# Full-width operands, ScalarE copies and closed chain visits in the RWKV stage of a decoder layer

## The chip, the cores and the metric

The kernel runs on one core of one Trainium2 chip. The metric is the device time of one execution in microseconds (us). The time before is 2257.15 us, the median of 3 runs (2256.23 to 2258.58).

## What is computed

One decoder layer on 1024 tokens of 1024 channels, in float32. One wide input projection of the normalised input feeds three branches and three gates per channel; the branches are merged, projected, and followed by a gated feed-forward network with a short convolution.

```python
h = rms_norm(x, norm_mix_pre)
z_pool, z_q, z_rwkv, z_gate = split(h @ w_in)        # 512, 512, 3328, 3072 columns
y_pool = pool_branch(z_pool) @ w_proj_pool           # causal means over 2, 4, 8, 16 tokens
y_mem  = mem_attention(z_q, mem, w_mem_kv) @ w_proj_mem   # 4 heads, 256 memory tokens
y_rwkv = rwkv_branch(token_shifted(z_rwkv)) @ w_proj_rwkv # 16 heads of 64 channels
merged = g0 * y_pool + g1 * y_rwkv + g2 * y_mem      # g = sigmoid(z_gate + gate_b)
x = x + rms_norm(merged @ w_o)
x = x + rms_norm(conv_ffn(rms_norm(x)))              # 1024 -> 2 x 2816 -> 1024

# rwkv_branch, for each head and token:
sa    = state @ an
state = state * w + outer(sa, bn) + outer(v, k)      # an = -kk, bn = kk * a
y     = state @ r
```

The RWKV recurrence over 1024 tokens is computed in 16 chunks of 64 tokens. Inside a chunk the recurrence becomes matrix products and the inverse of a triangular 64x64 matrix; between chunks the state is handed on.

## The kernel before

**Dense products.** Every float32 product is made of three fp32r matmuls (`mm3`, L158 to L163): operands are split into a high and a low part, and hi·hi, hi·lo and lo·hi are added in one accumulator. A block of the input projection (`in_block`, L249) is 128 output channels for all tokens: two halves of 512 tokens, eight input slices of 128, three matmuls each, so 48 matmuls of 128x512. Its weights come by DMA (`load_w`, L139), 128x256 at a time; `split_w` (L122) writes the high part, either on ScalarE (L124) where `hi_on_act` is set or on GpSimd (L126), and GpSimd subtracts for the low part (L127). Three raw and four split tiles of each class are kept in turn.

**Stages.** `start` (L316) makes the first blocks and the output gate of the RWKV branch. Then come four calls of `rwkv_group` (L376), one for each group of two pairs of heads (i = 0, 1; a pair fills 128 channels). After the groups: the keys and values of the memory, the attention (L643 to L714), the pool branch (L718 to L751), the projections of the three branches with the merge, the output projection, and the feed-forward network.

**A group.** Its parts, in the order of the program:
- preparation (L390 to L446): sigmoids of two low-rank products (psu, L398), the squared norm of the keys by a product with a matrix of ones for each head (`head_sums` L363, phd), a scan on VectorE, two exponentials, the block of r, then the operands AR (three planes: -kk decayed, r decayed, and a plane used by halves) and BK (L425 to L436, each by halves of 64 partitions), and the bonus r·k times v (pbo, L442), which goes to memory at L445;
- centred values (pv, L453 to L461);
- chunk products ps1 and ps2 (L469 to L489): 4 chunks a bank, two banks in turn, each read by three VectorE operations with a mask (L480 to L482, L487 to L489) into RB, NT and AR;
- BK times the chunk's decay Dc, one VectorE operation of 128x2048 for each pair (L491), transposes of it (pt) into BKN (L493 to L497);
- a recursion of 31 steps on VectorE that inverts 32x32 triangles (L513 to L518), between transposes (L510, L519, L520), then copies of the result into NT (L521 to L526), and the products pz and pw (L529 to L543) that join the halves of each 64x64 inverse;
- the chain of 16 chunks (L549 to L590). For each chunk: pr from the state (L554, L555), copied to Rs by VectorE (L557); pu = NT times Rs (L560, L561), copied to HV by VectorE and ScalarE (L566, L567); ph, the next state (L571, L572), added to the decayed one by VectorE (L577) for the next chunk; the output py in two parts, one that needs only the state (L564, L565) and one that needs pu (L586, L588), copied by ScalarE (L590). Each of these sets is eight small matmuls, 64 wide;
- the blocks of k and v of the next group (`group_kv`, L354), and the head norm of the outputs (pvar, L595 to L613).

**Order of the work.** Each engine runs a queue of its own. A scheduler orders the instructions of every engine by data, by free buffers and by their place in the program; `later` (L199) adds an order between two instructions without a wait of its own. The blocks that nobody in the groups needs (4 of the pool, 4 of the queries, 24 of the gates) stand in a list `fill`; the first 24 are written in the program behind the four groups, the last 8 in the pool stage (L739 to L741, two for each of the four pool groups gi). The scheduler takes their matmuls forward as filling wherever TensorE would have nothing to do.

**Pool stage.** For each gi: load z (tz, one buffer, so one gi after the other), window sums on VectorE over 128x1024 (L729 to L738), split into zh and zl for each half, three matmuls with the split pool weights (psg from zh, uhi), bias and scale, split again into ph_ and pl_, which the projection of the branch reads later.

## Time and profile before

| | us |
|---|---|
| median of 3 runs | 2257.15 |
| profiled execution: time | 2256.94 |
| profiled execution: span, first to last instruction | 2255.2 |
| TensorE busy | 2155.7 (96%) |
| VectorE busy | 1176.7 (52%) |
| ScalarE busy | 837.1 (37%) |
| GpSimd busy | 766.4 (34%) |
| mean granted clock of TensorE | 0.982 |

The profile is of one execution; its 2256.94 us lies 0.2 us below the median, and 1.7 us of it lie outside the span. A busy TensorE is not one at its peak: small matmuls, and matmuls at a lower clock, count as busy too. So the argument goes by three things: idle time of TensorE in front of a group of instructions and what released it, the distance from the start of one matmul to the start of the next, and the granted clock of a stretch.

### The profile page before, as it was taken

Reading aid. Unit: us, or ns where it says so; the run is one execution under the profiler, and the core shown is the slowest. Engines: PE = TensorE matmul, PEld = TensorE weight load, DVE = VectorE, ACT = ScalarE, POOL = GpSimd, SP = SyncE. Lnnn points to the kernel's source line nnn. Section 1 sums busy time; section 2 is a strip of 40 time slices with the busy share of each in tenths; the row PEclk is TensorE's granted clock in tenths of the full one; section 3 lists DMA queues with packets and bytes.
Section 4 is the critical chain, followed back from the end, with each engine's and each line's share of the span. In section 5 each row is a group of like instructions: output and inputs, shape, how many; then the busy total and the mean of one; then the engine's idle time right before and its main releaser. Section 6 shows DMA issues by size and latency. Waiting matters only on the chain.

```text
span 2255.2 us, 34230 instructions
## 1 busy us (share of the span) xinstructions
PE 2155.7 (96%) x12630; PEld 1649.1 (73%) x12630; DVE 1176.7 (52%) x2101; ACT 837.1 (37%) x1696; POOL 766.4 (34%) x1025
## 2 busy tenths in 40 slices
PE   7999899989998999899989999999999999999998
PEld 4767566766676667667877878777888888888887
DVE  6277539653965386634764442767403423334237
ACT  3342234223432252224634244545433413323143
POOL 6552116222521242212153355556422222323240
PEclk9999999999998999999999999999999999999999
DMA  4311112112111121114336343543211111111123
GB/s 138 126 54 50 38 60 68 57 39 67 66 55 41 54 92 44 57 56 142 98 117 201 130 145 100 163 153 94 76 50 45 50 50 42 54 40 57 38 75 136
DMA packets 147319, 181.46 MB, mean 80 GB/s; under 512 B 15824, under 2 KB 115792, under 8 KB 147152
## 3 DMA queue, kind: packets, MB, share of 16 engines
q1 hardware_dynamic: 147152, 179.28, 24.4%
q8 instruction: 100, 1.64, 0.3%
q14 instruction: 67, 0.55, 0.1%
HBM read 141.46 MB, written 37.75 MB: 79 GB/s over the span
## 4 chain that ended last, share of the span: by engine, by line
PE 73%; DVE 17%; DMA 3%; ACT 3%; issue 2%; POOL 2%; SPq 0%; POOLq 0%; ACTq 0%; DVEq 0%
PE psg L161 20%; PE psg L162 20%; PE psg L163 20%; DVE tb L518 2%; DVE tb L516 2%; PE ps L486 2%; PE ps L479 1%; POOL wlo L127 1%; PE pr L554 1%; PE pu L560 1%; ACT tHV L191 1%; DVE AR L425 1%; PE py L564 1%; PE py L586 1%; DMA wraw<-in_w_in 1%
## 5 line engine op out<-in xcount | busy, mean ns | idle before, releaser
L127 POOL TENSOR_TENSOR wlo<-wraw,whi 128x256 fp32r<-128x256 f32 (+1 forms) x696 | 578.3, 835 | 686.7 <-ACT whi L124 606.3
L161 PE MATMUL psg<-hh,whi 128*128 128x512 f32 x928 | 389.2, 420 | 0.9 <-ACT hh L117 0.7
L162 PE MATMUL psg<-hl,whi 128*128 128x512 f32 x928 | 386.6, 417 | 1.6 <-DVE hl L118 1.6
L126 POOL TENSOR_SCALAR whi<-wraw 128x256 fp32r<-128x256 f32 x240 | 151.3, 630 | 695.4 <-PE psg L162 671.9
L163 PE MATMUL psg<-hh,wlo 128*128 128x512 f32 x928 | 384.1, 414 | 0.2
L124 ACT CAST whi<-wraw 128x256 fp32r<-128x256 f32 (+1 forms) x488 | 191.8, 401 | 361.5 <-PE psg L162 274.2
L161 PE MATMUL psg<-h2h,whi 128*128 128x512 f32 x704 | 279.7, 397 | 4.4 <-DVE zc L826 4.4
L163 PE MATMUL psg<-h2h,wlo 128*128 128x512 f32 x704 | 278.7, 396 | 1.2 <-POOL wlo L127 1.2
L162 PE MATMUL psg<-h2l,whi 128*128 128x512 f32 x704 | 278.6, 396 | 0.0
L161 PEld LDWEIGHTS psg<-hh,whi 128*128 128x128 f32 x928 | 177.0, 191 | 47.0 <-issue 2.2
L163 PEld LDWEIGHTS psg<-hh,wlo 128*128 128x128 f32 x928 | 177.4, 191 | 43.2 <-issue 2.2
L162 PEld LDWEIGHTS psg<-hl,whi 128*128 128x128 f32 x928 | 177.0, 191 | 43.0 <-DVE hl L118 2.5
L161 PEld LDWEIGHTS psg<-h2h,whi 128*128 128x128 f32 x704 | 132.4, 188 | 37.3 <-ACT whi L124 5.0
L163 PEld LDWEIGHTS psg<-h2h,wlo 128*128 128x128 f32 x704 | 132.3, 188 | 34.2 <-POOL wlo L127 1.6
L162 PEld LDWEIGHTS psg<-h2l,whi 128*128 128x128 f32 x704 | 132.4, 188 | 32.7 <-issue 0.5
L823 DVE SCALAR_TENSOR_TENSOR uv<-psg,pv,uv 128x511 f32<-128x511 f32 x44 | 33.0, 749 | 156.7 <-ACT uv L822 156.7
L163 PE MATMUL psg<-fh,wlo 128*128 128x512 f32 x288 | 113.8, 395 | 0.0
L162 PE MATMUL psg<-fl,whi 128*128 128x512 f32 x288 | 113.8, 395 | 0.0
L161 PE MATMUL psg<-fh,whi 128*128 128x512 f32 x288 | 113.6, 395 | 0.0
L823 DVE SCALAR_TENSOR_TENSOR ug<-psg,pv,ug 128x511 f32<-128x511 f32 x44 | 32.9, 749 | 146.2 <-ACT ug L822 146.2
L989 DVE TENSOR_TENSOR acc<-acc,psg 128x512 f32<-128x512 f32 x48 | 33.0, 687 | 102.5 <-PE psg L163 102.5
L276 ACT ACTIVATE st<-psg,pv 128x512 f32<-128x512 f32 x48 | 33.1, 690 | 108.9 <-PE psg L163 99.1
(341 smaller groups left out, 3975.0 us busy)
## 6 DMA issues: line engine op xcount, KB each, us to landing
wraw<-in_w_in SPq DMA_DIRECT2D x240, 128.0 KB, 2.3
wraw<-in_w_fup SPq DMA_DIRECT2D x216, 128.0 KB, 2.3
d_zg<-st SPq DMA_DIRECT2D x48, 256.0 KB, 2.6
wraw<-in_w_fdn SPq DMA_DIRECT2D x80, 128.0 KB, 2.1
wraw<-in_w_prwkv SPq DMA_DIRECT2D x64, 128.0 KB, 2.3
wraw<-in_w_o SPq DMA_DIRECT2D x64, 128.0 KB, 2.3
xr<-in_xT SPq DMA_DIRECT2D x16, 256.0 KB, 5.4
d_g<-st SPq DMA_DIRECT2D x16, 256.0 KB, 2.0
```

What stands on the lines that cost most here:

```text
L124: A.copy(hi, src)
L126: G.tensor_scalar(hi, src, 1.0, 0.0, op0=ALU.mult, op1=ALU.add)
L127: (V if lo_on_dve[0] else G).tensor_tensor(lo, src, hi.bitcast(F32), op=ALU.subtract)
L161: first = PE.matmul(ps, wh, xh, start=start, stop=False)
L162: PE.matmul(ps, wh, xl, start=False, stop=False)
L163: last_mm[0] = PE.matmul(ps, wl, xh, start=False, stop=stop).ins
L276: A.activation(st, ps, AF.Identity, bias=bias)
L486: PE.matmul(ps[:, c], BK[i][up, c0 + c], AR[up, i, 1:3, t], start=True, stop=True)
L516: V.tensor_tensor(tm, X[:, s + 1:, s:s + 1].broadcast_to([P, n, m]), S[:, s:s + 1, 0:m].broadcast_to([P, n, m]), op=ALU.mult)
L518: V.tensor_tensor(S[:, s + 1:, 0:m], S[:, s + 1:, 0:m], tm, op=ALU.add)
L823: V.scalar_tensor_tensor(d[:, 1:], ps[:, :511], col("cw1", j), d[:, 1:], op0=ALU.mult, op1=ALU.add)
L989: V.tensor_tensor(accs[n][:, j], accs[n][:, j], ps, op=ALU.add)
```

## The change

Eight edits, all but two of them inside `rwkv_group`:

1. `square_sums` takes the place of `head_sums`: ScalarE writes the rounded square and the full square, two operations of 128x512 for each half, where it wrote one square of 128x1024 and VectorE rounded it.
2. The products for AR and BK are made for 128 rows in one operation (AR: 4 VectorE operations become 2; BK: 4 become 2, with one result first in t2), and ScalarE copies halves of 64 rows to where they are needed: one for AR and three for BK, for each pair.
3. `product_bank`: ps1 and ps2 take three banks in turn. RB is copied by ScalarE without the mask, and VectorE masks it later in four operations of 128x1024 in front of the chain. The bonus (pbo) moves behind the products of i = 0.
4. BK times Dc: 16 ScalarE operations of 128x128 for i = 0; 8 of them and a VectorE operation on the other half for i = 1.
5. `fill_to(95 * g + 95)`: six blocks of `fill` are written into each group in front of the NT copies. The order behind the recursion is moved: only the first pz matmul is ordered, behind the last NT copy of VectorE.
6. `visit`: the small matmuls of a chunk are tied together by `later`: pr with the first part of py, pu alone, ph with the second part of py. pr, pu and ph take two banks in turn.
7. `hi_on_act` is set after `start`, and stays: the high parts of nearly all weights are written by ScalarE (L124), where in the groups and in the pool stage GpSimd wrote them.
8. The 24 blocks behind the groups are gone (edit 5 has them), and the pool stage takes the 8 that are left, two for each gi as before.

The diff, cut to its core:

```diff
+    def square_sums(src, scale, sq):
...
-            V.tensor_copy(sp[:, n, 0], src[:, s])
-            V.tensor_tensor(sp[:, n, 1], src[:, s], sp[:, n, 0].bitcast(F32), op=ALU.subtract)
+            A.activation(sp[:, n, 0], src[:, s], AF.Square, scale=scale)
+            A.activation(sq[:, s], src[:, s], AF.Square, scale=scale)
+            V.tensor_tensor(sp[:, n, 1], sq[:, s], sp[:, n, 0].bitcast(F32), op=ALU.subtract)
...
+            A.copy(AR[64:128, i, 2], AR[64:128, i, 0])
             V.tensor_tensor(t5_, t5_, t4_, op=ALU.mult)
-            V.tensor_tensor(BK[0:64, :, 0:64], c3(t5_)[0:64], c3(t2_)[0:64], op=ALU.mult)
-            V.tensor_tensor(BK[64:128, :, 64:128], c3(t5_)[64:128], c3(t2_)[64:128], op=ALU.mult)
+            V.tensor_tensor(BK[:, :, 0:64], c3(t5_), c3(t2_), op=ALU.mult)
+            A.copy(BK[64:128, :, 64:128], BK[64:128, :, 0:64])
...
+            V.tensor_tensor(t2_, t4_, t2_, op=ALU.mult)
+            A.copy(BK[0:64, :, 64:128], c3(t2_)[0:64])
+            A.copy(BK[64:128, :, 0:64], c3(t2_)[64:128])
...
-                V.tensor_tensor(RB[i][:, 0, cs], ps[:, :, 1], bc(mincl, full), op=ALU.mult)
+                A.copy(RB[i][:, 0, cs], ps[:, :, 1])
...
-            V.tensor_tensor(BK[i], BK[i], Dc[:, i].unsqueeze(2).broadcast_to([P, NCH, P]),
-                            op=ALU.mult)
+            for b in range(2 if i == 0 else 0):
+                bonus(b)
+            n = NCH if i == 0 else 8
+            for c in range(n):
+                A.activation(BK[i][:, c], BK[i][:, c], AF.Identity, scale=Dc[:, i, c:c + 1])
...
-        behind = V.transpose(X.rearrange("p u t -> p t u"), S).ins
+        V.transpose(X.rearrange("p u t -> p t u"), S)
+        fill_to(95 * g + 95)
...
+        for i in range(2):
+            for e in range(2):
+                V.tensor_tensor(RB[i][:, e], RB[i][:, e], mincl.unsqueeze(1).broadcast_to([P, NCH, C]),
+                                op=ALU.mult)
...
+            visit(row, ready)
...
+    first_kv = start()
+    hi_on_act[0] = True
...
-    for j, ev in fill[:24]:
-        in_block(j, ev, 1)
...
-            n = 16 + 2 * gi
-            for j, ev in gates[n:n + 2]:
+            for j, ev in fill[2 * gi:2 * gi + 2]:
                 in_block(j, ev, 1)
```

How the orders of the engines move is shown at three places. **TensorE in the chain**, before: one chunk in the first group (hh, hl: the normalised input; psg: a dense block). The small sets stand in visits of their own between dense matmuls.

```order
L162 MATMUL psg<-hl,whi 128x512
L564 MATMUL py<-AR,HV 64x64
L565 MATMUL py<-AR,HV 64x64
L564 MATMUL py<-AR,HV 64x64
L565 MATMUL py<-AR,HV 64x64
L163 MATMUL psg<-hh,wlo 128x512
L554 MATMUL pr<-HV,AR 64x64
L555 MATMUL pr<-HV,AR 64x64
L554 MATMUL pr<-HV,AR 64x64
L555 MATMUL pr<-HV,AR 64x64
L161 MATMUL psg<-hh,whi 128x512
```

The same place of the change; here L589 is the line of `visit`, through which all the small matmuls go, and L161 to L163 are the dense ones as before:

```order
L162 MATMUL psg<-hl,whi 128x512
L589 MATMUL pr<-HV,AR 64x64 x4
L589 MATMUL py<-AR,HV 64x64 x4
L163 MATMUL psg<-hh,wlo 128x512
L589 MATMUL pu<-Rs,NT 64x64 x4
L161 MATMUL psg<-hh,whi 128x512
L162 MATMUL psg<-hl,whi 128x512
L163 MATMUL psg<-hh,wlo 128x512
L161 MATMUL psg<-hh,whi 128x512
L589 MATMUL ph<-HV,BKN_1303 64x64 x2
```

The first part of py now stands with pr in one visit; a chunk has three visits where it had four. The same table gives the number of dense matmuls between the last chunk product of a group and its first pz: 123 before, 226 in the first group and 211 to 213 in the others in the change.

**TensorE in the pool stage**, before, around the products of the third pool group (zh, zl): dense blocks of the input projection stand between them and after them.

```order
L161 MATMUL psg<-hh,whi 128x512
L161 MATMUL psg<-zh,uhi 128x512
L162 MATMUL psg<-hl,whi 128x512
L163 MATMUL psg<-hh,wlo 128x512
L162 MATMUL psg<-zl,uhi 128x512
L163 MATMUL psg<-zh,ulo 128x512
L161 MATMUL psg<-hh,whi 128x512
```

In the change, from the third pool group to the fourth (ph_, pl_: the finished pool outputs, read by the branch's projection; oh: the attention's output, read by its projection):

```order
L161 MATMUL psg<-zh,uhi 128x512
L162 MATMUL psg<-zl,uhi 128x512
L163 MATMUL psg<-zh,ulo 128x512
L161 MATMUL psg<-ph__9400,whi 128x512
L162 MATMUL psg<-pl__9401,whi 128x512
L163 MATMUL psg<-ph__9400,wlo 128x512
L161 MATMUL psg<-ph__9400,whi 128x512
L162 MATMUL psg<-pl__9401,whi 128x512
L163 MATMUL psg<-ph__9400,wlo 128x512
L161 MATMUL psg<-zh,uhi 128x512
```

From the first to the last of these pool products there were 192 matmuls of the input projection before and there is 1 in the change; 114 matmuls of the pool's projection are taken forward to there, and the last zh stands only six matmuls behind the third.

**ScalarE in the preparation of the second pair**, in the change, from the rounding of weights to the first chunk product's copy:

```order
L124 CAST whi<-wraw 128x256 x3
L438 COPY AR<-AR 64x1024
L444 ACTIVATE tHV<-tHV,oka,pv 128x1024
L442 COPY BK_5328<-BK_5328 64x16x64
L262 ACTIVATE AR<-psg,omu 128x512
L124 CAST whi<-wraw 128x256
L447 COPY BK_5328<-tBN_5325 64x16x64
L448 COPY BK_5328<-tBN_5325 64x16x64
L124 CAST whi<-wraw 128x256 x3
L262 ACTIVATE AR<-psg,omu 128x512
L497 COPY RB_5689<-ps_5709 128x256
```

Before, at the same place and up to the first copy of a centred value:

```order
L124 CAST whi<-wraw 128x256
L276 ACTIVATE st<-psg,pv 128x512
L433 ACTIVATE tHV<-tHV,oka,pv 128x1024
L276 ACTIVATE st<-psg,pv 128x512
L444 ACTIVATE kv_5784<-kv_5784,pv 128x1024
L460 COPY HV<-pv 64x8x64
```

Four copies of halves and the rounding of all weights have come into ScalarE's queue in front of the copies that free the product banks.

More of the change, by code (lines that the diff above doesn't have):

```diff
@@ L174, in gemm @@
                 later(m, behind)
+            if log is not None:
+                log.append(last_mm[0])
         return ps
@@ L401, in rwkv_group, with product_bank @@
         vs = []
+        turn = [0]
+        def product_bank(name):
+            turn[0] = (turn[0] + 1) % 3
+            shape = [P, 4, 2, C]
+            return pss.tile(shape, F32, name=name, tag="s") if turn[0] else \
+                psk.tile(shape, F32, name=name, tag="k")
         for i in range(2):
@@ L548, in rwkv_group, with bank, visit @@
         Hd = rw.tile([P, 2, C], F32, name="Hd", tag="Hd")
+        turn = [0]
+        def bank(name):
+            turn[0] ^= 1
+            return (psc if turn[0] else psk).tile([P, 2, C], F32, name=name, tag="c" if turn[0] else "k")
+        def visit(products, after):
+            for (out_, l, r), kw in products:
+                m = PE.matmul(out_, l, r, **kw)
+                if after is not None:
+                    later(m, after)
+                after = m.ins
+            return after
@@ L568, in rwkv_group @@
+            for i in range(2):
+                kw = dict(start=c == 0 and i == 0, stop=i == 1)
+                row.append(((py[lo, i], HV[:, i, c, 0], RB[i][:, 0, c]), kw))
+                row.append(((py[up, i], HV[:, i, c, 1], RB[i][:, 1, c]), kw))
+            visit(row, ready)
             if c + 1 < NCH:
-                ph = psc.tile([P, 2, C], F32, name="ph", tag="c")
-                for i in range(2):
-                    PE.matmul(ph[lo, i], BKN[i][:, c, 0:64], HV[:, i, c, 0], start=True, stop=True)
-                    PE.matmul(ph[up, i], BKN[i][:, c, 64:128], HV[:, i, c, 1], start=True, stop=True)
```

112 lines of the change are left out of this document (61 added, 51 removed).

## The prediction, on record before the run

> **What bounds the kernel now.** I read the page's busy shares first, then the busy time of each engine in the stretches of the groups, the groups of instructions with what ended the idle time before them, and TensorE's timeline at one place of each kind.
>
> ```profile
> PE 2155.7 (96%) x12630; PEld 1649.1 (73%) x12630; DVE 1176.7 (52%) x2101; ACT 837.1 (37%) x1696; POOL 766.4 (34%) x1025
> ```
>
> ```profile
> 113.00:339.00 226.00, 215.27 (x1728) 153.10 (x1728) 138.21 (x274) 75.44 (x152) 66.29 (x91) 0.98 0.15 50
> ...
> sum 902.00, PE 852.03 PEld 608.65 DVE 562.52 ACT 303.93 POOL 267.18; mean PE 213.01 PEld 152.16 DVE 140.63 ACT 75.98 POOL 66.79
> ```
>
> TensorE is busy for 96% of the span; no other engine passes 52%. The four stretches are one group's period each (chain to chain); in them TensorE idles 902.00 − 852.03 = 50 us. So a gain can come from idle TensorE time, from time that it is busy for badly, and from nothing else; a relieved VectorE is worth only what waits for it. The groups say what waits:
>
> ```profile
> L534 PE MATMUL pz<-tb,NT 32*32 32x32 f32 x512 | 12.5, 214 | 30.3 <-DVE tb L519 30.3
> L442 PE MATMUL pbo<-kv,bonesr 128*128 128x512 f32 x32 | 15.9, 618 | 12.6 <-DVE kv L438 12.6
> L398 PE MATMUL psu<-ld,ulo 128*128 128x512 f32 x16 | 6.9, 430 | 2.8 <-POOL ulo L313 2.8
> L161 PE MATMUL psg<-hh,whi 128*128 128x512 f32 x700 | 298.0, 426 | 0.1
> ```
>
> The end of VectorE's recursion (before pz) and the bonus's operand account for 42.9 of the 50 us; the dense matmuls wait for nothing. A gap also costs behind itself. This is TensorE behind the first recursion:
>
> ```profile
> 240.99 1.92 PE L534 MATMUL pz<-tb,NT 32*32 32x32 f32 x64 [7.46 <-DVE tb L519]
> ...
> 243.43 0.63 PE L162 MATMUL psg<-hl,whi 128*128 128x512 f32 x1
> 243.86 0.63 PE L163 MATMUL psg<-hh,wlo 128*128 128x512 f32 x1
> ```
>
> and the granted clock (the third number from the end) in the stretches there:
>
> ```profile
> 240.00:246.00 6.00, 5.01 (x72) 3.97 (x73) 5.00 (x7) 2.99 (x5) 1.23 (x2) 0.50 0.01 3
> 246.00:252.00 6.00, 6.00 (x138) 4.14 (x137) 2.27 (x5) 3.63 (x7) 1.14 (x2) 0.80 0.26 90
> ```
>
> Behind the 7.46 us gap the granted clock is 0.50, then 0.80 in the next 6 us, and dense matmuls start 0.43 us apart (243.43 to 243.86). Next, one chunk of the chain:
>
> ```profile
> 287.34 0.40 PE L162 MATMUL psg<-hl,whi 128*128 128x512 f32 x1
> 287.66 0.27 PE L564 MATMUL py<-AR,HV 64*64 64x64 f32 x1
> ...
> 288.06 0.50 PE L163 MATMUL psg<-hh,wlo 128*128 128x512 f32 x1
> 288.49 0.27 PE L554 MATMUL pr<-HV,AR 128*64 128x64 f32 x1
> ...
> 288.72 0.22 PE L555 MATMUL pr<-HV,AR 128*64 128x64 f32 x1
> 288.87 0.51 PE L161 MATMUL psg<-hh,whi 128*128 128x512 f32 x1
> 289.21 0.39 PE L162 MATMUL psg<-hl,whi 128*128 128x512 f32 x1
> 289.44 0.40 PE L163 MATMUL psg<-hh,wlo 128*128 128x512 f32 x1
> ```
>
> Dense matmuls in a run start 0.23 us apart (289.21 to 289.44). From 287.34 to 289.21 there are three dense steps, 0.70 us, and the visits of py and pr; so the two visits cost 1.87 − 0.70 = 1.17 us, though their 16 small matmuls start within 0.25 us of each other in each visit. The rest is the way in (0.09 more than a dense step), the way out (0.15, from 288.72 to 288.87) and a first dense step that is 0.11 too long (0.34).
>
> **The change part by part.** *Cover for the recursion (edit 5).* The last product eviction of the first group, and pz:
>
> ```profile
> 203.48 0.42 DVE L489 TENSOR_TENSOR AR<-ps,mstrict 64x256 f32<-64x256 f32 x1
> 203.82 2.27 DVE L491 TENSOR_TENSOR BK<-BK,Dc 128x2048 f32<-128x2048 f32 x1
> ```
>
> From 203.5 to 240.99 are 37.5 us, and TensorE had 123 dense matmuls for them by its order: 123 × 0.233 = 28.7 us and the transposes, 7.5 short, as the trace has it. The change puts 211 to 226 there, 49 to 53 us. The NT copies that now stand ahead of pz add some 3.5 us to the 37.5, so about 8 us remain to spare: the gap goes, −30.3 us. With it goes the slow clock: 5 us at 0.50 and 6 us at 0.80 lose 2.5 + 1.2 = 3.7 us at most; I take 3.0 a group, since the time to change modes may not scale with the clock: −12.
>
> *Bonus (edit 3).* pbo now stands behind the products of i = 0, long after its operand: −12.6 us. The short wait before psu goes with GpSimd's rounding of weights: −2.8, rounded to −3.
>
> *Visits (edit 6).* py's first part joins pr. What stays inside is a step from pr's matmuls (128x64) to py's (64x64). This trace shows that step where the two happened to meet:
>
> ```profile
> 328.12 0.22 PE L555 MATMUL pr<-HV,AR 128*64 128x64 f32 x1
> 328.27 0.27 PE L565 MATMUL py<-AR,HV 64*64 64x64 f32 x1
> ```
>
> 0.15 us, the same as the way out to a dense matmul. So a merged visit saves 0.09 + 0.15 + 0.11 of one visit and pays 0.15: 0.20 us, in 60 chunks (four groups, fifteen with a first py) −12 us. The Trainium skill, "TensorEngine Tiling (Array Packing)", Key Properties, says that a change of tiling mode drains the array while a change of tile does not. The row agrees that the switch inside the visit costs as much as one at its end; counted as if only visits cost, the saving would be 0.35 × 60 = 21 us. Elsewhere in the groups about 20 more switches go, at 0.15: −3.
>
> *What ScalarE takes over (edits 1 to 4, 7).* Its prices, and what VectorE and GpSimd give up:
>
> ```profile
> L126 POOL TENSOR_SCALAR whi<-wraw 128x256 fp32r<-128x256 f32 x171 | 106.7, 624 | 575.5 <-PE psg L162 558.7 <-issue 12.7 <-POOL ulo L313 1.9
> L124 ACT CAST whi<-wraw 128x256 fp32r<-128x256 f32 x4 | 1.6, 402 | 0.5 <-PE psg L162 0.5
> L480 DVE TENSOR_TENSOR RB<-ps,mincl 128x256 f32<-128x256 f32 x32 | 13.6, 425 | 54.2 <-PE ps L479 54.1
> L410 ACT ACTIVATE tHV<-kv,pv 128x1024 f32<-128x1024 f32 x6 | 6.9, 1152 | 0.0
> L584 ACT ACTIVATE Hd<-Hn,Dc 128x64 f32<-128x64 f32 x112 | 32.9, 340 | 34.8 <-DVE Hn L582 32.6 <-DVE Hn L580 2.2
> ```
>
> ```profile
> 330.00:397.00 67.00, 62.15 (x300) 44.97 (x299) 55.26 (x65) 34.23 (x49) 35.94 (x34) 0.97 0.22 78
> ```
>
> For each group: 43 roundings at 0.402 = 17 us; 16 copies of RB at 0.40 = 6.4; 8 copies of halves at 1.15 = 9.2; 24 scalings by Dc at about 0.34 = 8.2; squares +2.5. That is 43 us on top of 76 in a period of 225, so ScalarE is not full over a group. In the preparation it comes close: in the 67 us from 330 it had 34 and gets some 20 more, in a stretch that should itself shrink to about 60. VectorE is paid there: 16 evictions × 0.425 = 6.8 and the 2.27 us of L491 among others go, and four masks of 128x1024 come back.
>
> What this costs TensorE the trace of before doesn't show. From below it is nothing: TensorE's dense filling covers all of it. From above, every one of the 16 product banks of a group is freed late by two roundings that stand ahead of the copy, 16 × 0.8 = 13 us. I take half of the banks late by one rounding, 8 × 0.40 = 3.2, and two copies of halves (2 × 1.15 = 2.3) on the path from VectorE's operand to the first product: 5.5 us a group, +22. It lies nearer to nothing because three banks in turn give slack that two did not. The Trainium skill, "ScalarE: Activation LUTs", Rules for kernel authors, tells to keep plain multiplications on VectorE. By its about 0.3 us for each instruction and 0.83 ns for each element, my estimate for a 128x128 scaling is 0.41 us, 24 of them 9.8 us against the two VectorE operations that L491 measures at 2.27; no run here shows that shape, and the sum, by the row, has 8.2.
>
> *Pool stage (edits 5 and 8).* The filling is taken from here.
>
> ```profile
> 1141.00:1212.00 71.00, 65.42 (x262) 50.08 (x261) 41.50 (x55) 21.39 (x36) 40.71 (x45) 0.95 0.39 132
> ```
>
> ```profile
> 1141.98 0.69 DVE L118 TENSOR_TENSOR ol<-po,oh 128x512 fp32r<-128x512 f32 x1 [1.57 <-ACT oh L117]
> 1165.63 0.50 PE L161 MATMUL psg<-zh,uhi 128*128 128x512 f32 x1 [3.65 <-ACT zh L117]
> 1183.26 0.50 PE L161 MATMUL psg<-zh,uhi 128*128 128x512 f32 x1 [1.85 <-ACT zh L117]
> 1200.41 0.89 DVE L118 TENSOR_TENSOR zl<-tz,zh 128x512 fp32r<-128x512 f32 x1 [0.74 <-ACT zh L117]
> ```
>
> The attention ends at 1142. VectorE, one pool group after another, has the second zh at 1165.6, the third at 1183.3, the fourth at 1200.4: some 58 us that no edit shortens. TensorE had 37 + 192 dense matmuls of the input projection and 29 others for it, and waited 5.5 us in all (3.65 + 1.85). By the new order it has 37 + 1 dense ones and 138 others, 176 × 0.233 = 41 us, and the projection of the attention's output stands behind the last zh. So it waits 58 − 41 = 17, and pays one slow clock of 3: 20 in place of 5.5 and the slow clock behind it (the stretch's 0.95), about +12. From below +5 (a faster VectorE), from above +20.
>
> *Sum*, against the profiled execution's 2256.94 us, 0.2 below the median: −30.3 − 12 − 12.6 − 3 − 12 − 3 = −72.9; +22 + 12 = +34; −39. Forecast 2218 us.
>
> **The rivals.**
> *Clean.* No new wait in the groups. For it: dense matmuls waited 0.1 us in all, and VectorE gains more than counted. In the recursion its steps stretch when GpSimd works:
>
> ```profile
> 212.22 0.82 DVE L516 TENSOR_TENSOR tb<-tb 128x87 f32<-128x87 f32 x1
> 213.35 0.35 DVE L516 TENSOR_TENSOR tb<-tb 128x112 f32<-128x112 f32 x1
> ```
>
> The smaller operation took 0.82 us, 0.47 longer than the larger one; 107 us less of GpSimd's rounding (L126) would take many such stretches out of the preparation. The Trainium skill, "SBUF — State Buffer", SBUF: two separate sides, says that the port pair that VectorE and GpSimd share is locked for a whole instruction; the two rows agree in size: the stretch is near the 0.62 us of L126's row. Against it: the preparation's ScalarE queue. Time: 2257 − 72.9 + 12 = 2196. Chance 0.24.
>
> *Heavy.* Banks and copies cost their upper bound, 12 us a group, and the pool stage 20: −72.9 + 68 = −5, 2252 us. Chance 0.16.
>
> *Slower: the chain waits behind roundings.* GpSimd's rounding spent 558.7 us waiting for a matmul to free its tile (L126's row). In ScalarE's queue this wait stands ahead of the copy of pu and of Hd, and both lie on the chain.
>
> ```profile
> 290.26 0.28 DVE L566 COPY HV<-pu 64x128 f32<-64x128 f32 x1
> 290.58 0.26 ACT L567 COPY HV<-pu 64x128 f32<-64x128 f32 x1 [1.30 <-DVE HV L566]
> 291.50 0.27 PE L586 MATMUL py<-RB,HV 128*64 128x64 f32 x1
> ```
>
> The copy ends at 290.84; 0.38 us of slack is my estimate for the new order. A rounding that waits for three dense steps (0.70) and takes 0.40 makes 1.10, 0.72 beyond the slack; at both places of 60 chunks that is 86 us: 2257 − 39 + 86 = 2304. It decides from 39 / 120 = 0.33 us at each place. Against it: the scheduler places the copies, and ScalarE is at a third of its time in the chain. Chance 0.07.
>
> *The gap stays.* The six blocks stand ahead of pz but their weights come too late, and TensorE waits as before: −72.9 + 30.3 + 12 + 34 = +3, 2260 us. Against it: 12 dense matmuls (2.8 us) use one 128x256 weight tile, which costs ScalarE 0.40. Chance 0.05.
>
> **How the numbers follow.** The forecast, 0.48, holds 2207 to 2235; clean 0.24, below; heavy 0.16, 2235 to 2256. A measurement of this kernel tells 0.2%, 4.5 us, from no change. Slower by over that: 0.08, from the chain and part of the gap case; within: 0.06, from the ends of heavy and gap; faster 0.86. The range, 2188 to 2247, leaves out the end of clean (0.04) and, above, the end of heavy with the last two (0.16).
>
> **What would show it.** Right: no idle time before pz (L558) and pbo, a clock of 1.0 behind the recursion, about 2.4 us net for the visits of a chunk, some 17 us of idle TensorE before the last zh matmuls, ScalarE at about 120 us a group. Wrong: idle time before pu or ph in the chain released by ScalarE; more than 13 us a group before the products; or idle time before pz that is still 7 us.

## The result, and the profile after

| | before | changed |
|---|---|---|
| median, us | 2257.73 (2256.23 to 2258.58, 4 runs) | 2221.78 (2218.92 to 2227.2, 4 runs) |
| profiled execution: span | 2255.2 | 2218.8 |
| TensorE busy | 2155.7 | 2133.7 |
| TensorE idle in the span | 99.5 | 85.1 |
| mean granted clock | 0.982 | 0.986 |

The ratio is 0.9844, with a 95% interval of 0.9824 to 0.9865: faster, by 36 us or 1.6%. Of the 36.4 us between the two spans, 14.4 are idle time of TensorE that went, and 22.0 are busy time that went though the number of its matmuls is the same (12630).

The groups of instructions of the changed kernel, in the stretch of the four RWKV groups (113 to 1015 us), that answer to those quoted of before; behind the second bar stands the idle time ahead of a group and what ended it:

```profile
L163 PE MATMUL psg<-hh,wlo 128*128 128x512 f32 x748 | 310.6, 415 | 7.5 <-POOL wlo L127 7.1
L161 PE MATMUL psg<-hh,whi 128*128 128x512 f32 x749 | 309.6, 413 | 15.9 <-ACT whi L124 15.9
L460 PE MATMUL pbo<-kv,bonesr 128*128 128x512 f32 x32 | 16.5, 617 | 1.3 <-DVE AR L499 0.9 <-ACT BK L512 0.4
L558 PE MATMUL pz<-tb,NT 32*32 32x32 f32 x512 | 9.6, 192 | 0.0
L548 ACT COPY NT<-tb 32x512 f32<-32x512 f32 x16 | 9.8, 615 | 40.3 <-DVE tb L543 40.2
```

The wait before pz is gone (30.3 us before), that before pbo nearly (12.6 before). The dense matmuls, which waited for nothing, now wait 15.9 us for high parts of weights and 7.1 for low parts. The last row says why: ScalarE stands still 40.3 us in front of its copies of the recursion's result into NT. ScalarE's timeline in the first group, and then TensorE's:

```profile
215.60 0.41 ACT L124 CAST whi<-wraw 128x256 fp32r<-128x256 f32 x1 [0.99 <-PE psg L162]
224.59 0.62 ACT L548 COPY NT<-tb 32x512 f32<-32x512 f32 x1 [8.58 <-DVE tb L543]
225.11 0.57 ACT L276 COPY st<-psg 128x512 f32<-128x512 f32 x1
225.59 0.40 ACT L124 CAST whi<-wraw 128x256 fp32r<-128x256 f32 x1
```

```profile
220.96 0.40 PE L163 MATMUL psg<-hh,wlo 128*128 128x512 f32 x1
226.04 0.50 PE L161 MATMUL psg<-hh,whi 128*128 128x512 f32 x1 [4.69 <-ACT whi L124]
226.38 0.45 PE L162 MATMUL psg<-hl,whi 128*128 128x512 f32 x1
226.97 0.79 PE L163 MATMUL psg<-hh,wlo 128*128 128x512 f32 x1
```

ScalarE reaches its NT copy at 216 and waits there for the recursion until 224.59. Behind the copy stand an eviction and a rounding (L124). TensorE uses up the rounded weights by 221 and starts again at 226.04, right behind that rounding. It happens once in each group: 4.69, 3.32, 4.11 and 3.74 us. TensorE does not wait for the recursion any more, but for an engine that waits for it.

The wait for low parts comes in the preparation, once in each of the last three groups. TensorE and GpSimd there:

```profile
372.59 0.40 PE L162 MATMUL psg<-hl,whi 128*128 128x512 f32 x1
375.35 0.50 PE L163 MATMUL psg<-hh,wlo 128*128 128x512 f32 x1 [2.36 <-POOL wlo L127]
...
376.61 0.49 PE L162 MATMUL psg<-hl,whi 128*128 128x512 f32 x1
376.91 0.63 PE L163 MATMUL psg<-hh,wlo 128*128 128x512 f32 x1
377.33 0.63 PE L161 MATMUL psg<-hh,whi 128*128 128x512 f32 x1
```

```profile
367.19 8.10 POOL L127 TENSOR_TENSOR wlo<-wraw,whi 128x256 fp32r<-128x256 f32 x6 [20.86 <-ACT whi L124]
```

GpSimd had waited 20.86 us for a high part (ScalarE was busy with the preparation), then made six low parts in 8.10 us.

One visit of the chain as it now is, pr and the first part of py together:

```profile
267.83 0.39 PE L161 MATMUL psg<-hh,whi 128*128 128x512 f32 x1
268.20 0.45 PE L589 MATMUL pr<-HV,AR 128*64 128x64 f32 x8
268.58 0.45 PE L589 MATMUL py<-AR,HV 64*64 64x64 f32 x8
268.96 0.50 PE L162 MATMUL psg<-hl,whi 128*128 128x512 f32 x1
269.38 0.45 PE L589 MATMUL pu<-Rs,NT 64*64 64x64 f32 x8
```

From 267.83 to 268.96 are 1.13 us; less a dense step of 0.23, they leave 0.90. The next dense step, from 268.96 to 269.38, takes 0.42: 0.23, the 0.09 of the way into a visit, and 0.10 that it is too long. With this 0.10 the visit costs 1.00 us, where the two visits of before cost 1.17. The pool stage:

```profile
1140.00:1202.00 62.00, 45.86 (x155) 31.38 (x155) 41.57 (x61) 27.15 (x52) 17.85 (x20) 0.84 0.46 148
1198.10 0.79 PE L161 MATMUL psg<-zh,uhi 128*128 128x512 f32 x1 [7.22 <-ACT zh L117]
```

TensorE idles 16.1 of 62 us (5.6 of 71 before), and the clock is 0.84 (0.95 before).

### The profile page after: what moved, and what is told of

Same layout as the page of the kernel before. It is cut to its first block, busy times and chain, and to the rows that moved or that the text cites. A ratio compares the mean times of both kernels' runs of the same rounds, so it can differ in the third digit from the quotient of the medians.

```text
span 2218.8 us, 34334 instructions
## 1 busy us (share of the span) xinstructions
PE 2133.7 (96%) x12630; PEld 1638.3 (74%) x12630; DVE 1103.2 (50%) x2001; ACT 1010.0 (46%) x2132; POOL 616.1 (28%) x805
## 4 chain that ended last, share of the span: by engine, by line
PE 45%; DMA 2%; DVE 2%; ACT 1%; POOL 1%; issue 1%; SPq 0%; ACTq 0%; POOLq 0%; DVEq 0%
PE psg L161 14%; PE psg L162 14%; PE psg L163 14%; POOL wlo L127 1%; DMA g<-d_zg 1%; DMA wraw<-in_w_kv 0%; PE ptr L765 0%; DMA wraw<-in_w_o 0%; DVE o L981 0%; DMA wraw<-in_w_pmem 0%; DVE o L983 0%; DVE s L942 0%; PE po L161 0%; DMA pm<-d_zg 0%; PE psco L161 0%
## 5 line engine op out<-in xcount | busy, mean ns | idle before, releaser
L127 POOL TENSOR_TENSOR wlo<-wraw,whi 128x256 fp32r<-128x256 f32 (+1 forms) x696 | 565.1, 818 | 1463.7 <-ACT whi L124 1344.0
L124 ACT CAST whi<-wraw 128x256 fp32r<-128x256 f32 x704 | 276.3, 402 | 467.0 <-PE psg L162 340.7
L161 PE MATMUL psg<-hh,whi 128*128 128x512 f32 x928 | 381.0, 411 | 17.0 <-ACT whi L124 15.9
L163 PE MATMUL psg<-hh,wlo 128*128 128x512 f32 x928 | 382.7, 413 | 7.5 <-POOL wlo L127 7.1
L162 PE MATMUL psg<-hl,whi 128*128 128x512 f32 x928 | 380.6, 410 | 1.3 <-DVE hl L118 1.3
L161 PE MATMUL psg<-h2h,whi 128*128 128x512 f32 x704 | 279.5, 397 | 3.3 <-ACT whi L124 3.3
L163 PE MATMUL psg<-h2h,wlo 128*128 128x512 f32 x704 | 278.9, 396 | 1.3 <-POOL wlo L127 1.3
L161 PEld LDWEIGHTS psg<-hh,whi 128*128 128x128 f32 x928 | 176.2, 190 | 59.9 <-ACT whi L124 17.6
L163 PEld LDWEIGHTS psg<-hh,wlo 128*128 128x128 f32 x928 | 176.2, 190 | 56.4 <-POOL wlo L127 16.0
L161 PEld LDWEIGHTS psg<-h2h,whi 128*128 128x128 f32 x704 | 132.4, 188 | 36.3 <-ACT whi L124 3.7
L163 PEld LDWEIGHTS psg<-h2h,wlo 128*128 128x128 f32 x704 | 132.3, 188 | 34.3 <-POOL wlo L127 1.8
L163 PE MATMUL psg<-fh,wlo 128*128 128x512 f32 x288 | 113.8, 395 | 0.0
L161 PE MATMUL psg<-fh,whi 128*128 128x512 f32 x288 | 113.7, 395 | 0.0
L633 DVE TENSOR_TENSOR HV<-ph,Hd 64x128 f32<-64x128 f32 x112 | 32.3, 289 | 71.9 <-PE ph L589 44.9
L161 PEld LDWEIGHTS psg<-fh,whi 128*128 128x128 f32 x288 | 54.2, 188 | 13.1
```

Of the source, the lines that this page charges most:

```text
L124: A.copy(hi, src)
L127: (V if lo_on_dve[0] else G).tensor_tensor(lo, src, hi.bitcast(F32), op=ALU.subtract)
L161: first = PE.matmul(ps, wh, xh, start=start, stop=False)
L162: PE.matmul(ps, wh, xl, start=False, stop=False)
L163: last_mm[0] = PE.matmul(ps, wl, xh, start=False, stop=stop).ins
L633: ready = V.tensor_tensor(HV[q, :, c + 1, e], ph[q], Hd[q], op=ALU.add).ins
```

## The experiments

Theory: in the changed kernel ScalarE's queue decides in the groups, at one place, the NT copies, since whatever stands behind them waits for the recursion. The rival of the prediction's working: ScalarE costs time at the product banks and at the copies of halves. Each kernel is the changed one with the edit shown, or, where its heading names an earlier experiment, that one with it; the medians of before in the three sets of runs are 2256.22, 2259.75 and 2256.57 us. Differences in us are of medians; taken by the ratios, each to the before of its own set, they come out up to 3 us otherwise. For the comparison of stretches, "beyond dense" is the length of a stretch by the starts of TensorE's matmuls, less 0.233 us for each dense matmul of the input projection in it.

**e1: the NT copies on VectorE.**

```diff
-                if q % 2 == 0:
-                    A.copy(NTu[qs, us, bs], X[qs, us])
-                else:
-                    place = V.tensor_copy(NTu[qs, us, bs], X[qs, us]).ins
+                place = V.tensor_copy(NTu[qs, us, bs], X[qs, us]).ins
```

> All eight copies of the recursion's result into NT are made by VectorE, so that ScalarE has nothing in its queue that waits for the recursion. Theory (ScalarE, stuck at its NT copy, holds back the rounding of weights behind it, and the dense matmuls run out of high parts): the four gaps before a dense matmul during the recursion (4.69, 3.32, 4.11, 3.74 us, 15.9 in all) go, and with them a few us of slow clock; about 2203 us. Rival (GpSimd's subtraction is what is short, ScalarE's wait only coincides): the same idle time comes back before the lo matmuls; 2220 us.

2196.61 us, ratio 0.9725 (0.9699 to 0.9751). No wait of the dense matmuls for high parts is left; the one for low parts stays:

```profile
L161 PE MATMUL psg<-hh,whi 128*128 128x512 f32 x731 | 299.9, 410 | 0.0
L163 PE MATMUL psg<-hh,wlo 128*128 128x512 f32 x730 | 300.3, 411 | 7.3 <-POOL wlo L127 7.1
```

25 us for four copies of 0.6 us a group put elsewhere: 15.9 of idle time, and busy time at a low clock behind it. From the last product to pz, beyond dense falls from 9.1, 7.8, 8.1 and 7.6 us in the four groups to 2.3, 2.3, 2.2 and 2.2, 23.6 in all. The theory holds, and the gain was larger than the 19 it expected.

**e2: GpSimd rounds the weights as before.**

```diff
-    hi_on_act[0] = True
     kv = group_kv(0, [first_kv])
...
-        lo_on_dve[0] = True
+        hi_on_act[0] = lo_on_dve[0] = True
...
-        lo_on_dve[0] = False
+        hi_on_act[0] = lo_on_dve[0] = False
...
+    hi_on_act[0] = True
```

> Edit 7 alone undone: GpSimd rounds the high parts in the groups and in the pool stage as before, all else as changed. Theory (the same as above: ScalarE's queue is the new bound of the groups): the four gaps of 15.9 us in the recursions go and no others of that size come; about 2203 us. Rival (the rounding was moved with reason: GpSimd's 107 us slow VectorE down, and preparation and products come later): 2222 us or more, with idle time before pv, the products or pbo of 4 us a group.

2212.04 us, ratio 0.9806 (0.977 to 0.9842): between the two expectations; the interval overlaps the changed kernel's. The dense matmuls still stop. One of the places, on TensorE and on ScalarE:

```profile
456.20 0.79 PE L161 MATMUL psg<-hh,whi 128*128 128x512 f32 x1 [5.67 <-ACT st L278]
```

```profile
453.70 1.87 ACT L548 COPY NT<-tb 32x512 f32<-32x512 f32 x3 [13.59 <-DVE tb L543]
455.48 0.67 ACT L278 ACTIVATE st<-psg,pv 128x512 f32<-128x512 f32 x1
```

Now it is a finished block's bank that stands behind the NT copy: TensorE waits for its eviction (st). So the theory's first form, that the rounding is what is held up, was too narrow; anything behind that copy is. The wait for low parts in the preparation is down from 7.1 to 1.9 us, so it came with ScalarE's rounding; e9 shows what else had a part in it. The rival, that GpSimd's rounding slows the preparation, fails, though its mechanism is there: by the trace the recursion takes 36.6 to 38.1 us (34.8 to 35.0 in the changed kernel) and pv waits 4.1 us in all, but the dense matmuls cover the former, and the kernel is not slower.

**e3: the last eight blocks kept for the memory and the pool stage.**

```diff
-            PE.matmul(pmm[:, :256], ones, sq, start=k == 0, stop=k == KC - 1)
+            pm_ = PE.matmul(pmm[:, :256], ones, sq, start=k == 0, stop=k == KC - 1).ins
+            if k == 0:
+                held = [pm_]
...
+    held.append(last_mm[0])
...
-                in_block(j, ev, 1)
+                in_block(j, ev, 1, behind=held[gi // 2])
```

> The last eight filling blocks are kept from being taken forward into the groups: four are ordered behind the first matmul of the memory's norm, four behind the attention. In the order, the pool stage has 197 dense matmuls of the input projection again (1 as changed), the groups 200 fewer, and pz the same 211 to 226 ahead of it. Theory (the filling was moved to where TensorE was busy anyway, and its place in the pool stage stayed empty): the idle time before the zh and ph matmuls (some 15 us) falls to about 5 and the groups don't idle more; about 2208 us. Rival (the blocks covered other waits in the groups, and what is given back to the pool stage is lost there): 2220 us.

2247.26 us, ratio 0.9958 (0.9941 to 0.9975): 25 us slower than the changed kernel, a miss beyond the rival's price. The pool stage did get its cover back: it idles 5.8 us, where the changed kernel idles 16.1. The chain of the last group lost it; there, in this kernel and in the changed one:

```profile
944.00:1015.00 71.00, 52.00 (x681) 41.56 (x682) 22.66 (x78) 21.84 (x69) 0.00 (x0) 0.50 0.09 31
1031.79 1.65 PE L710 MATMUL pmm<-msq,ones 128*128 128x256 f32 x3 [15.87 <-ACT msq L709]
```

```profile
944.00:1006.00 62.00, 61.53 (x752) 40.92 (x750) 20.58 (x72) 22.77 (x71) 5.82 (x8) 1.00 0.11 36
```

No group follows the fourth, so its chain has no blocks of k and v to run between its visits. The changed kernel had taken 109 dense matmuls of the last eight blocks there. Without any, the chain lasts as long (61.1 us, 61.6 with them), at a clock of 0.50, and TensorE idles 15.87 us behind it (2.33 in the changed kernel). The filling that the prediction saw as taken from the pool stage was covering this.

**e4: the chain as before.** The loop of before (L549 to L590 there) in place of `bank` and `visit`:

```diff
-            pr = bank("pr")
+            pr = psc.tile([P, 2, C], F32, name="pr", tag="c")
...
-            visit(row, ready)
+                PE.matmul(pr[lo, i], AR[ke, i, 0, t], HV[ke, i, c, 0], start=True, stop=True)
```

> Edit 6 alone undone: the chain is written as before, with py's first part, pr, pu and ph in visits as the scheduler puts them, all in the bank pool of before. Theory (a visit costs its way in and out): about 0.2 us a chunk more, +12 to +13; 2234 us. Rival (the merged visits only moved time that the dense matmuls cover, or the gain came from pr, pu and ph having two banks and no waits): 2221 us, or more than 2240 with idle time before pr, pu or ph.

2243.86 us, ratio 0.9951 (0.9935 to 0.9966): 22 us slower than the changed kernel. Beyond dense, the chain (last pw to last pr) takes 39.5, 39.6, 39.6 and 40.8 us; 35.9, 35.5, 35.5 and 36.1 in the changed kernel: 16.5 us. So edit 6 is worth more than the 12 to 13 counted for its visits. The rival's waits are not there: the rows of pr, pu and ph have no idle time in e4 (0.0 each). What the second bank does alone was not tried, and the rest of the 22 is not settled by this run.

**e5: e1 and e2 together.**

> e1 and e2 together: VectorE makes the NT copies and GpSimd rounds the weights in the groups. In e2 the dense matmuls still stopped during the recursion (4.69, 5.67, 5.54, 1.96 us), now behind a block's copy to memory that stood behind ScalarE's NT copy. Theory (whatever stands behind ScalarE's NT copy holds back the dense matmuls; the rounding is only one such thing): these 17.9 us go and some slow clock with them; about 2191 us. Rival (GpSimd's rounding slows VectorE, and that decides once ScalarE is free): no better than e1, 2197 us or more.

2190.15 us, ratio 0.9693 (0.9678 to 0.9707). The 17.9 us of e2 are gone: with ScalarE out of the recursion, the eviction is free as well. GpSimd's rounding does no harm. The interval still overlaps e1's at its edge, so a gain over e1 is not shown by the time.

**e6: e1 with five blocks a group.**

```diff
-        fill_to(95 * g + 95)
+        fill_to((79, 159, 239, 319)[g])
...
-            for j, ev in fill[2 * gi:2 * gi + 2]:
+            for j, ev in fill[3 * gi:3 * gi + 3]:
```

> e1 with five filling blocks a group in place of six ahead of pz, and twelve in place of eight written in the pool stage. In the order pz has 163 to 178 dense matmuls ahead of it (211 to 226 in e1), the groups 2408 in all (2600), the pool stage 193 (1). Theory (the sixth block was more than the recursion needed, and e3 lost because it took the blocks from the last group's chain, not from there): the idle time in the pool stage falls to about 5 us, pz does not wait, no wait comes at the end of the last group; about 2185 us. Rival (the recursion needs the cover: 163 matmuls are 38 us, and the copies of NT come later): pz waits some 3 us a group and the gain is gone; 2196 us.

2207.53 us, ratio 0.9774 (0.9754 to 0.9793): slower than e1 by 11 us, and a miss beyond the rival's 2196. The pool stage does fall to 4.9 us of idle time, as the theory has it. The rival is right that the recursion needs the cover, but pz does not wait. In the second group, TensorE and VectorE behind the recursion, and the granted clock:

```profile
446.19 0.39 PE L162 MATMUL psg<-hl,whi 128*128 128x512 f32 x1
448.18 1.10 PE L563 MATMUL pw<-NT,tb 32*32 32x32 f32 x57 [1.60 <-DVE tb L559]
```

```profile
443.20 3.88 DVE L547 COPY NT<-tb 32x512 f32<-32x512 f32 x8
447.11 0.29 DVE L609 COPY Rs<-pr 128x128 f32<-128x128 f32 x1
447.43 0.70 DVE L559 COPY tb<-pz 32x512 f32<-32x512 f32 x1
```

```profile
452.00:458.00 6.00, 6.00 (x74) 4.17 (x74) 0.00 (x0) 0.58 (x1) 0.00 (x0) 0.50 0.01 3
458.00:464.00 6.00, 6.00 (x30) 3.63 (x29) 0.66 (x3) 0.84 (x2) 0.00 (x0) 0.52 0.00 0
```

VectorE's eight NT copies end at 447.1, so pz's result is copied late and pw waits 1.60 us. The clock falls to 0.50 and stays there for over 12 us. Beyond dense, pz to the last pw goes from 6.6 to 11.1 us and more, and the chain from between 35.5 and 36.2 to between 38.3 and 38.7, in each of the last three groups. 163 to 165 dense matmuls are too few here.

**e7: e5 with five blocks a group.**

> e5 and e6 together (NT copies by VectorE, rounding in the groups by GpSimd, five blocks a group). If both theories hold their gains add: about 2179 us. If GpSimd's rounding slows VectorE so that the recursion outlasts 175 to 195 dense matmuls, pz waits and it is 2190 us or more.

2177.69 us, ratio 0.9639 (0.962 to 0.9658). With GpSimd rounding, the scheduler puts 175 to 195 dense matmuls ahead of pz. Beyond dense, pz to the last pw takes 6.6, 7.2 and 7.2 us, so 181 are nearly enough; in the last group, which has the 175, it takes 9.8.

**e8: the filling as before.**

```diff
-        fill_to(95 * g + 95)
...
-                    if u0 == u == 0:
-                        later(m, place)
+                    later(m, behind)
...
     lr_ctx.close()
+    fill_to(95 * 3 + 95)
```

> Edit 5 (with 8) alone undone: the 24 blocks are written behind the groups, pz is ordered behind the recursion's last transpose as before. Theory (the prediction's sum): pz waits 7 us a group again and the slow clock comes back, +42; the pool stage gets its cover back, -12; the dense matmuls do not stop at ScalarE's NT copy, since pz does in any case, -16 to -20: about 2234 us. Rival (the edit's gain is far less than the gap, since its cover is only taken from elsewhere): 2222 us.

2238.29 us, ratio 0.9905 (0.989 to 0.992): 16.5 us slower than the changed kernel (14 by the ratios). The wait before pz is back where it was:

```profile
L557 PE MATMUL pz<-tb,NT 32*32 32x32 f32 x512 | 12.5, 214 | 28.6 <-DVE tb L542 28.6
L161 PE MATMUL psg<-hh,whi 128*128 128x512 f32 x701 | 291.6, 416 | 1.0 <-ACT whi L124 0.9
L163 PE MATMUL psg<-hh,wlo 128*128 128x512 f32 x700 | 293.5, 419 | 9.7 <-POOL wlo L127 9.5
```

pz waits 28.6 us, and the dense matmuls hardly wait for high parts any more (1.0 us); the wait for low parts stays (9.7). Edit 5 removes a wait of 28.6 and, at ScalarE's NT copy, makes one of 15.9.

**e9: the halves of AR and BK by VectorE.** L425 to L436 of before in place of the full-width products and ScalarE's copies.

> Edit 2 alone undone: VectorE makes the four halves of AR and BK for each pair as before, and ScalarE copies none. The prediction put two of these copies (2.3 us a group) on the path to the products as a cost of the change. If that is so, undoing takes up to 9 us off: 2213 us. The theory now (ScalarE cost time only where it waited for the recursion; its copies stand under cover, and VectorE is what the products wait for): VectorE gets some 9 us a group more ahead of the products, the preparation takes longer by that and the dense matmuls cover only a part: 2222 to 2240 us.

2230.1 us, ratio 0.988 (0.9865 to 0.9895): 8 us slower, with an interval that touches the changed kernel's at its edge. The products wait for VectorE:

```profile
L502 PE MATMUL ps<-AR,BK 64*128 64x128 f32 x256 | 41.1, 302 | 17.5 <-DVE AR L498 17.5
```

In the changed kernel this wait is 0.9 us. pbo waits for nothing in e9 (0.0), so with the halves on VectorE the bonus's new place only moves the wait from pbo to the products; it takes edit 2 to remove it. On the way to the products, then, the copies are no cost. They seem to have one elsewhere, which the time of the whole hides. In e9 the dense matmuls hardly wait for low parts, where they wait 7.5 us in the changed kernel:

```profile
L163 PE MATMUL psg<-hh,wlo 128*128 128x512 f32 x742 | 305.9, 412 | 0.7 <-POOL wlo L127 0.4
```

In the changed kernel's second group, the four copies of the first pair (L438, L442, L447, L448; 1.04 to 1.05 us each) stand in ScalarE's queue ahead of the rounding that GpSimd waits for. The last two of them and the rounding:

```profile
363.43 1.04 ACT L447 COPY BK<-tBN 64x1024 f32<-64x1024 f32 x1
364.49 1.04 ACT L448 COPY BK<-tBN 64x1024 f32<-64x1024 f32 x1
...
366.67 0.40 ACT L124 CAST whi<-wraw 128x256 fp32r<-128x256 f32 x1
```

GpSimd's wait of 20.86 us there is 12.93 in e9. The order of the dense matmuls moves with this edit too, so how much of the 6.8 us is the copies' is not shown. Edit 2 as a whole is a gain of some 8 us, at the edge of what the times tell apart.

**e10: RB masked out of the bank by VectorE.**

```diff
-                A.copy(RB[i][:, 0, cs], ps[:, :, 1])
+                V.tensor_tensor(RB[i][:, 0, cs], ps[:, :, 1], mincl.unsqueeze(1).broadcast_to([P, 4, C]), op=ALU.mult)
...
-        for i in range(2):
-            for e in range(2):
-                V.tensor_tensor(RB[i][:, e], RB[i][:, e], mincl.unsqueeze(1).broadcast_to([P, NCH, C]),
-                                op=ALU.mult)
```

> The part of edit 3 that concerns RB undone: VectorE reads RB from the product banks with the mask, as before, and the four masks of 128x1024 ahead of the chain are gone; the three banks stay. The prediction charged 3.2 us a group for banks that ScalarE frees late: if so, 2209 us. The theory now (three banks hide it; VectorE's third operation for each bank makes the products longer): 2222 to 2232 us.

2211.28 us, ratio 0.9793 (0.9776 to 0.9809): 10 us faster. The number is the one that the prediction's working gives, the way is another:

```profile
L161 PE MATMUL psg<-hh,whi 128*128 128x512 f32 x763 | 316.2, 414 | 8.9 <-ACT whi L124 8.9
L548 ACT COPY NT<-tb 32x512 f32<-32x512 f32 x16 | 9.9, 617 | 33.0 <-DVE tb L543 32.9
```

The products take as long as before the edit (beyond dense 26.2 to 28.6 us; 26.3 to 28.9 in the changed kernel). ScalarE's wait at the NT copy is 33.0 us for 40.3, and the dense matmuls' 8.9 for 15.9: 7 us less of each. By the trace the recursion's first transpose starts 3.7 to 4.2 us behind the last product (5.3 to 5.8 in the changed kernel, where two masks of 128x1024, 1.56 and 1.22 us in the first group, stand ahead of it on VectorE). That the order of the masks is the reason is read from the trace, not tried by itself.

**e11: BK times Dc on VectorE.**

```diff
-            n = NCH if i == 0 else 8
-            for c in range(n):
-                A.activation(BK[i][:, c], BK[i][:, c], AF.Identity, scale=Dc[:, i, c:c + 1])
...
+            V.tensor_tensor(BK[i], BK[i], Dc[:, i].unsqueeze(2).broadcast_to([P, NCH, P]),
+                            op=ALU.mult)
```

> Edit 4 alone undone: one VectorE operation of 128x2048 for each pair multiplies BK by Dc, as before, and ScalarE's 24 scalings a group (0.393 us each in the changed kernel, 9.4 us a group) are gone. If ScalarE's load matters in the products: up to 9 us a group, 2200 us. The theory now (ScalarE matters only at its NT copy): the recursion starts some 2 us later for VectorE's 3.3 us, ScalarE's wait and the stop of the dense matmuls behind it grow by that; 2222 to 2230 us.

2226.29 us, ratio 0.9857 (0.9838 to 0.9876); the interval overlaps the changed kernel's, so no difference is shown by the time. ScalarE's wait grew to 46.5 us, and the dense matmuls' to 16.8:

```profile
L544 ACT COPY NT<-tb 32x512 f32<-32x512 f32 x16 | 9.8, 612 | 46.5 <-DVE tb L539 46.3
```

The recursion starts 6.7 to 7.7 us behind the last product (5.3 to 5.8 in the changed kernel), as expected. ScalarE has 9.4 us less to do in each group, and that is no gain: it only waits the longer.

**e12: e7 with six blocks in the last group.**

```diff
-        fill_to((79, 159, 239, 319)[g])
+        fill_to((79, 159, 239, 335)[g])
```

> e7 with six filling blocks ahead of the last group's pz in place of five, and eleven in place of twelve written in the pool stage. In e7 the last group alone lost time behind its recursion (9.8 us beyond the dense matmuls from pz to the last pw, 6.6 in the first; 39.6 in the chain, 35.5 in the others). Theory (175 dense matmuls are too few there): these 7 us come back, and the pool stage loses 48 matmuls of cover, some 3 us: 2174 us. Rival (the pool stage needs the block as much): 2178 us.

2171.89 us, ratio 0.9628 (0.9612 to 0.9645). The last group's stretch from pz to pw is 6.6 us again, its chain 35.9. The fastest kernel here, 50 us under the changed one; its interval overlaps that of e7.

## Why the prediction was right, and where its working was not

The forecast, 2218 us, is 4 us under the median and 2.6 under the profiled execution of the changed kernel. The signs that it named came too: no idle time before pz, a clock of 1.00 behind the first recursion (240 to 258), 2.2 us beyond dense for the visits of a chunk, ScalarE busy for 108 to 122 us a group. Step by step:

- *The gap before pz*, −30.3: right, 30.3 to 0.0, and e8 brings 28.6 back.
- *The slow clock behind it*, −12: 10.5, by beyond dense from pz to the last pw (9.4, 9.3, 9.6 and 8.6 before, 6.6 each after).
- *The bonus*, −12.6: 11.3 (12.6 to 1.3). But e9 shows that the new place alone does not do it: with edit 2 undone pbo waits 0.0 and the products 17.5. The term belongs to edits 2 and 3 together, and the prediction gave it to edit 3. *psu*, −3: that row waits 0.1 us after 2.8, but the four psu rows together 1.2 after 3.3, so 2.1.
- *The visits*, −12 and −3: the single visit was well sized (0.97 us expected for the merged one, 1.00 measured, so 10 us for 60). The chain as a whole gained 17 us beyond dense (40.7, 40.3, 40.2 and 39.0 to 35.9, 35.5, 35.5 and 36.1), and e4 gives 16.5 for edit 6 alone. The mechanism stands, and the term was some 2 to 5 us too small.
- *New waits in the groups*, +22: 23.0 by the rows (15.9 and 7.1), and some 31 with the low clock behind the stops (e1's 23.6 beyond dense, and 7.1); but not where the prediction put them. This is the step that failed: "half of the banks late by one rounding, 8 × 0.40 = 3.2, and two copies of halves (2 × 1.15 = 2.3) on the path from VectorE's operand to the first product". The products of the changed kernel wait 0.9 and 1.6 us in all groups together. e10, which takes ScalarE's part of the banks away, leaves the products as they are, and e9, which takes the copies away, makes the products wait 17.5 us. If the copies cost something, then by the rounding behind them, on the way to the dense matmuls' low parts (7.5 us, 0.7 in e9). What the prediction missed above all is one line of its own part on edit 5: it counted the NT copies as 3.5 us of delay for pz, and did not ask what is queued behind ScalarE's half of them while it waits for the recursion. e1 shows that wait to be worth 25 us. That the forecast size is near the rows' 23.0 is chance.
- *The pool stage*, +12: 10.5 us of idle time (5.6 to 16.1) and a lower clock (0.84 of 62 us, 0.95 of 71): 10 and 3.6 us lost by the clock, some of it while idle. From the first to the last pool product, less 0.233 us for each 128x512 matmul of psg, 10.5 us became 25.9, so the term measures +15 and +12 was a little low. What the filling did in exchange was not seen: e3 shows that the chain of the last group, which has no blocks of its own, needed it.
- *The sum*: idle time −30.3 − 12.6 − 3 + 22 + 11.5 = −12 was forecast (11.5 from the pool stage's 17 in place of 5.5), and −14.4 measured; busy time −27 and −22.0. Beyond dense, the four groups (from 113 us to the last pr) went from 422.6 to 373.6 us: −49, where −72.9 + 22 = −51 was forecast. So the total is right because the net of the groups and the pool stage are each nearly right. But inside the groups the waits cost some 9 us more than forecast, and the gains came to some 80 us, of which the terms above name 71; where the other 9 lie is not settled by these runs.

*The rivals.* The clean case had VectorE gain from a GpSimd that rounds less. The trace shows the stretching: in the changed kernel's second group VectorE's operations of 128x1024 take 1.63 to 1.74 us while GpSimd makes its six low parts, and 1.21 to 1.23 ahead of that. The Trainium skill, "SBUF — State Buffer", SBUF: two separate sides, has the two engines lock a port pair against each other. GpSimd's low parts take 1.35 us each there and 0.74 alone (at 378.95), so these times agree that each holds the other up; that one waits out a whole instruction of the other they do not show. In e2 the stretching is worth 1.7 to 3.3 us of each recursion. But e2 and e5, which give the rounding back to GpSimd, are not slower than the changed kernel and e1 (medians 10 and 6 us lower, intervals that overlap), so it did not set the time. The slower rival, roundings ahead of the chain's copies, did not come: pr, pu and ph wait 0.8 us in all, and the dense matmuls, not the chain, met ScalarE's queue. The gap before pz did not stay (0.0). ScalarE's scalings by Dc take 0.393 us in the trace after, where the sum had 0.34 from another shape's row. The estimate from the Trainium skill, "ScalarE: Activation LUTs", Rules for kernel authors, was 0.41 and lay nearer. The advice of the same section of the Trainium skill, to keep such products on VectorE, did not decide here: by e11, following it changes nothing that can be measured.

## What to carry to other kernels

When filling is put in front of a wait, look for every other instruction that waits for the same event, and at what stands behind it on its engine: here a copy of 0.6 us on ScalarE held up weights and banks that the filling needed, and moving four of them a group gained 25 us. Filling that a scheduler spreads by itself covers more places than the one it is taken from; before holding it back, find the stretch that has none of its own (here the chain of the last group). When a product that waits is moved later, ask what will wait for the same engine in its place: with the halves on VectorE the bonus's wait only moved to the chunk products. A sum can come out right with a term in the wrong place, so a term that the trace of before cannot show deserves its experiment even then.

## What the runs showed of the hardware

A short gap of TensorE can be followed by a low clock, and the same gap can be followed by none. In the changed kernel a gap of 2.36 us stands before a low part in each of the last three groups. Behind the first, dense matmuls start 0.23 us apart for 1.3 us and then, from 376.91, 0.42 to 0.43 apart for seven steps. Behind the other two (606.23 and 835.61) they start 0.23 apart throughout; the first of these, and two steps from where the slow ones would be:

```profile
606.23 0.50 PE L163 MATMUL psg<-hh,wlo 128*128 128x512 f32 x1 [2.36 <-POOL wlo L127]
...
607.73 0.40 PE L163 MATMUL psg<-hh,wlo 128*128 128x512 f32 x1
607.96 0.39 PE L161 MATMUL psg<-hh,whi 128*128 128x512 f32 x1
```

In e1 it is the first of the three that has no slow steps, and the other two have seven each. So the length of the gap does not decide alone; what does, these runs do not show.

Among matmuls of 32x32 and of 64 columns the price was higher. In e6 a gap of 1.60 us there was followed by a clock of 0.50 for over 12 us; in e7, at the same place, a gap of 0.59 was followed by none (1.00 from 442 to 454). In its last three groups e6 idles 5.7 us before pw, where e1 does not idle, and takes some 23 us more beyond dense from pz to the end of the chain. No idle time shows this price: over their whole spans e6 idles no more than e1 (67.3 and 67.9 us), and is 11 us slower.
